# A two-block fp32 network on one Trainium2 core: transposes of normed tiles later in TensorE's order at two handoffs, and one modulation part moved to the second layer's mixer

## The chip, the cores and the metric

The kernel runs on one core of one Trainium2 chip. The metric is the device time of one execution in microseconds (us), as the median of several runs; lower is better. The program is one launch, with all weights in device memory (HBM) at its start.

## The reference, cut to what matters

A sequence of 256 rows of width 1024 goes through two hybrid layers (a mixer of pooling and sparse attention, then a feed-forward block with squared ReLU), and then through one block of a state-space branch, a dilated attention branch and another feed-forward block. All values are fp32. Two things of it bear on the change: each hybrid layer normalises its input and scales, shifts and gates it by six vectors that come from a matrix product with the conditioning vector `c`, and the last block ends its first half with a layer norm.

```python
def first_block(x, c, w_mod, b_mod, ...):
    c_act = jax.nn.silu(c)
    for l in range(DEPTH):                       # 2 layers
        mod = c_act @ w_mod[l] + b_mod[l]        # 1024 -> 6 * 1024
        x = hybrid_layer(x, mod, ...)

def hybrid_layer(x, mod, norm1, norm2, w_in, ..., w_out, w_ff1, w_ff2):
    shift1, scale1, gate1, shift2, scale2, gate2 = jnp.split(mod[:, None, :], 6, axis=-1)
    h = rms_norm(x, norm1) * (1.0 + scale1) + shift1
    proj = h @ w_in
    ...
    x = x + gate1 * mix
    h2 = rms_norm(x, norm2) * (1.0 + scale2) + shift2
    ff = jnp.square(jax.nn.relu(h2 @ w_ff1)) @ w_ff2
    return x + gate2 * ff

def second_block(x, ...):
    ...
    h = layer_norm(alpha * h + mix, ln1_g_2, ln1_b_2)
    f = jnp.square(jax.nn.relu(h @ w_up_2)) @ w_down_2
    return layer_norm(alpha * h + f, ln2_g_2, ln2_b_2)
```

## The kernel before

**Products.** The 256 rows are two tiles of 128 rows, called t=0 and t=1. To keep fp32 accuracy each operand is split into a high and a low part, and each product is three matmuls (`wh,hl`, `wl,hh`, `wh,hh`; the helper `mm` is L89). Weights are read once from HBM, 250 MB in all, in loads of 512 KB.

**Weights.** `Weights.load` (L130) takes a staging buffer `wst` (five of them, `nst=5`), issues the load on SyncE's DMA queue (SP, L136), lets ScalarE (ACT) copy it into a slot `wh` (L144) and VectorE (DVE) write the rest into a slot `wl` (L145). There are nine slots. A staging buffer is free again when its L145 is done, a slot when TensorE (PE) has used it.

**Modulation.** `mod_part` (L559) makes one of the six vectors of a layer. Its matrix is eight loads (L567) that go into the same five staging buffers. Each is multiplied by a column of `c` and added to `macc` by one DVE instruction (L569); in a part called with `modp1=99`, as those of the second layer's mixer are, the first of the eight goes over ACT (L571) and GpSimd (POOL, L572) instead. For a scale or a shift eight small matmuls then sum over the partitions (x16 in the profile, `tr<-cst,macc`) and DVE makes the columns `mcol` (L599, L601). For a gate, matmuls with `ones_r` spread the sum over all rows and ACT copies it to `mgate` (L589).

**Who does which part when.** The table `MODS` (L36) deals the parts to the stages: the first `mf0` of the list (0,5), (1,1), (1,0), (1,2), (1,3), (1,4) are made during layer 0's feed-forward, the rest during layer 1's mixer ((l,q): layer and vector). A part's steps are pulled by the weight loads: each load adds `W.rate` to a sum, and each whole unit takes one step (`Weights.load`, end).

**Handoffs.** Where a stage ends, its callback normalises tile t: `rms` (L609) squares on ACT (L613), makes the reciprocal root on POOL (L119) between two small DVE instructions, and scales on DVE (L617, `xn`). `to_fm` (L474) transposes `xn` on PE into the banks `tr` and `pv` (L479), applies scale and shift (DVE L488, ACT L486) and splits the result into `hh` and `hl` (L103, L106). `rms_fm` (L620) does not call `to_fm` at once: `later(n, fn)` (L184) puts it off by n ticks. In the last, wide pass of a stage one tick is two weight rows of one tile and one half, which is six matmuls. At the layer norm in the last block (`done_ln1`, L1646) `to_fm` is called at once.

**Order.** The program is written in this order, and a scheduler of the framework then fixes the order of each engine's instructions and of each queue's transfers. At run time every engine takes its instructions strictly in that order. The rope tables of layer 1 (L681 to L684, some 30 small POOL instructions), the pooling bands (L720, three loads) and the compression weights (L723, four loads) are also made at the handoff from layer 0 to layer 1.

Of the kernel before, what the change touches and what calls it, by code (L numbers as in the profile page):

```python
# [24 lines left out]
ALPHA = 2.0 ** 0.25  # L25

SZ = 1024
TU = dict(nst=5, tabc=2, nw=9, nt2=24, raw=1, krest=2, qrest=4, pool2=1, c2=3, c3=1, c4=1, ln=3, uv='uv', pre=[1], nv=5, nv1=0, nv0=0, u0=19.5, du=0.7, ub=2, uc=4, c0=32.5, dc=0.1, w0=36, dw=0.5, comp=22, pool=27, dpool=2, cmpa=32, cmpb=34, dcmp=2, e1=1, e0=1, pta=2, ahead=3, modp=3, rf=0.95, r0=0, r0b=2, r1=0.8, r1b=1.2, rs=14, raw_=4, qrest_=6, u0_=19.5, du_=1.0, comp_=22, pool_=26, cmpa_=31, cmpb_=35, nv_=0, nv0_=0, w0_=32, dw_=0.8, order2='v0 qk0 qk1 qk2 v1 B C x0 z0 x1 z1 x2 z2 x3 z3 g2 g3 pa g0 g1 ps', fm0=148, dfm=9, dts=8, dcd=30, par0=10, par1=40, d0=50, dd=2, db=3, dc2=5, ss0=70, ds=5.6, scb=5, sx=3, sr=6, sg=3.5, sy=3.5, sn=8, mf0=5, modp1=99, rf1=0.5, pool2_=3, c3_=2, c4_=3, nv1_=2, dpool_=2, dcmp_=1, dc_=0.4, cap=4, ub_=2.5, c0_=32.5, pta_=4)
NST, NW = TU['nst'], TU['nw']
NT2, NT4, NS5 = TU['nt2'], 5, 20  # L30

ORDER2 = TU["order2"].split()

MODS = {("mix", 0): ((0, 2), (0, 3), (0, 4)), ("ff", 0): [(0, 5), (1, 1), (1, 0), (1, 2), (1, 3), (1, 4)][:TU["mf0"]],  # L36
        ("mix", 1): [(0, 5), (1, 1), (1, 0), (1, 2), (1, 3), (1, 4)][TU["mf0"]:], ("ff", 1): ((1, 5),)}
CONV2 = {"x0": 0, "x1": 4, "x2": 8, "x3": 12, "B": 16, "C": 20}
# [23 lines left out]
def tile_two_blocks(ctx: ExitStack, tc: tile.TileContext, I, out, stop=None, dbg=None):  # L62
# [12 lines left out]
    def bank(tag):  # L75
        return pp.tile([128, 512], FT, name=tag, tag=tag, bufs={"acc": 4, "st": 2, "tr": 1, "pv": 1}[tag])

    def t2(shape, name, dt=FT):
        assert math.prod(shape[1:]) <= 512
        return bp.tile(shape, dt, name=name, tag="t2", bufs=NT2)  # L80
# [20 lines left out]
    def split(hi, lo, src, eng=None):  # L101
        if eng is A:
            A.activation(hi, src, AF.Copy)  # L103
        else:
            V.tensor_copy(hi, src)
        V.tensor_tensor(lo, src, hi, op=OP.subtract)  # L106
# [77 lines left out]
    def later(n, fn):  # L184

        waiting.append([n, fn])
# [284 lines left out]
    def new_h():  # L471
        return (xp.tile([128, 8, S], FR, name="hh", bufs=1), xp.tile([128, 8, S], FR, name="hl", bufs=1))

    def to_fm(t, xn, hi, lo, sc=None, sh=None, whole=None):  # L474

        for kb in range(2):
            b = bank(("tr", "pv")[kb])
            for k in range(4):
                T.transpose(b[:, k * 128:(k + 1) * 128], xn[kb][:, k * 128:(k + 1) * 128], ident)  # L479
            src = b.rearrange("p (a b) -> p a b", a=4)  # L480
            if sc is not None:
                hf = t2([128, 4, 128], "hf")
                for k in range(4):
                    kk = kb * 4 + k
                    if kb:
                        A.activation(hf[:, k], src[:, k], AF.Identity, bias=sh[:, kk:kk + 1], scale=sc[:, kk:kk + 1])  # L486
                    else:
                        V.tensor_scalar(hf[:, k], src[:, k], sc[:, kk:kk + 1], sh[:, kk:kk + 1], op0=OP.mult, op1=OP.add)  # L488
                src = hf
            ks, tsl = slice(kb * 4, kb * 4 + 4), slice(t * 128, t * 128 + 128)  # L490
            split(hi[:, ks, tsl], lo[:, ks, tsl], src, A)
            if whole:
                A.activation(whole[kb][:, :, tsl], src, AF.Copy)
# [3 lines left out]
    for l in range(DEPTH):  # L497
# [3 lines left out]
        if l == 0:  # L501
            for k in range(0, 8, 2):
                for n in "qk":
                    W.specs.append(([wi[:, k:k + 2, cols[n][0]:cols[n][1]]], 2, 512))
        for n in "qk" + TU["uv"]:
            if l or n in "uv":
# [6 lines left out]
    g2 = {}  # L513
# [43 lines left out]
    MC = {}  # L557
# [51 lines left out]
    def rms(t):  # L609
        ss = small.tile([128, 4], FT, name="ss", bufs=4)  # L610
        xn = [t2([128, 512], "xn") for _ in range(2)]
        for n in range(2):
            A.activation(xn[n], xs[t][:, n * 512:(n + 1) * 512], AF.Square, accum_out=ss[:, n:n + 1])  # L613
        V.tensor_scalar(ss[:, 2:3], ss[:, 0:1], D * EPS, ss[:, 1:2], op0=OP.add, op1=OP.add)
        rsqrt(ss[:, 3:4], ss[:, 2:3], 1)
        for n in range(2):
            V.tensor_scalar(xn[n], xs[t][:, n * 512:(n + 1) * 512], ss[:, 3:4], math.sqrt(D), op0=OP.mult, op1=OP.mult)  # L617
        return xn

    def rms_fm(l, q0, hi, lo, t):  # L620

        xn = rms(t)
        later(TU["ln"], lambda: to_fm(t, xn, hi, lo, MC[l, q0 + 1], MC[l, q0]))

    def first_mod(c):

# [36 lines left out]
    def hybrid_layer(l, hilo, between, done):  # L663
# [363 lines left out]
        def done1(t):  # L1027
            if not hi2lo2:
                W.until((l, 3), (l, 4))
                hi2lo2.extend(new_h())  # L1030
            rms_fm(l, 3, *hi2lo2, t)
# [111 lines left out]
    h1, h2_, hw = [], [], []  # L1143
# [5 lines left out]
    def done0(t):  # L1149
        if not h1:  # L1150
            W.until((1, 0), (1, 1))
            h1.extend(new_h())
        rms_fm(1, 0, *h1, t)

    hybrid_layer(0, h0, between0, done0)
    if stop == "l0":
        for t in range(2):
# [22 lines left out]
    def Q(n):  # L1180
        a, w = QC[n]
        return par2[:, a:a + w]

    hi, lo = h2_
# [413 lines left out]
    for i, it in enumerate(items):  # L1598
        g, t, sub = it
# [37 lines left out]
    def ln_stat(t):  # L1637
        mv = small.tile([128, 4], FT, name="bmv", bufs=2)
        V.bn_aggr(mv[:, 0:2], bst[t])
        V.tensor_scalar(mv[:, 2:3], mv[:, 1:2], NEPS / ALPHA ** 2, None, op0=OP.add)  # L1640
        rsqrt(mv[:, 3:4], mv[:, 2:3], 1)
        return mv

    hh = []

    def done_ln1(t):  # L1646
        if not hh:
            hh.extend(new_h())
        mv = ln_stat(t)
        xn = [t2([128, 512], "xn") for _ in range(2)]  # L1650
        for n in range(2):
            V.tensor_scalar(xn[n], xs[t][:, n * 512:(n + 1) * 512], mv[:, 0:1], mv[:, 3:4], op0=OP.subtract, op1=OP.mult)
        to_fm(t, xn, *hh, Q("ln1g"), Q("ln1b"))
        for n in range(2):
            ns = slice(n * 512, (n + 1) * 512)
            G.tensor_tensor(xs[t][:, ns], xn[n], rows["ln1_g_2"][:, n], op=OP.mult)
            G.tensor_tensor(xs[t][:, ns], xs[t][:, ns], rows["ln1_b_2"][:, n], op=OP.add)

    accs = {(t, n): bank("acc") for t in range(2) for n in range(2)}
    W.cap = NW  # L1660
    run(g2["o"].wide(act_o, accs, True, (ev_ln(0.5 / ALPHA), done_ln1)))

    def done_ln2(t):
# [122 lines left out]
```

## Time and profile before

| what | value |
|---|---|
| median of three runs | 1257.55 us (1257.31 to 1259.05) |
| the profiled execution | 1257.41 us |
| its span in the trace | 1255.6 us |
| PE busy | 1171.6 us, 93% of the span |
| DVE busy | 870.8 us, 69% |
| ACT busy | 646.3 us, 51% |
| POOL busy | 239.6 us, 19% |
| mean granted clock of PE | 0.981 |
| mean HBM rate | 197 GB/s |

The span runs from the first to the last instruction that the trace holds; the time of the execution has some 1.8 us around it. A time such as 387.76 is counted from the span's start. Busy shares are means over the program: the stages around the change are read from the timeline, in which each line is an instruction (or a merged run of equal ones) with its start, its duration, and in brackets the idle time of its engine ahead of it with what ended that. The granted clock is given as a share of full speed.

### The profile page before, as it was taken

The numbers are of one execution on the slowest core, as the hardware profiler recorded it, in microseconds if no ns is written. First come the engines' busy times: TensorE is split into PE (matmuls) and PEld (weight loads), VectorE is DVE, ScalarE is ACT, GpSimd is POOL, SyncE is SP. The second block draws the span as 40 slices with busy tenths as digits, with TensorE's granted clock in tenths as the row PEclk, the third lists the DMA queues.
The fourth block names the chain that finished last, engine by engine and source line by source line (L and its number), as shares of the span: only waits on it lengthen the run. The fifth ranks groups of instructions, "written<-read, shape, count | busy, mean of one in ns | idle before, by whom it ended". The sixth has DMA issues, their size and how long they took to land.

```text
span 1255.6 us, 18822 instructions
## 1 busy us (share of the span) xinstructions
PE 1171.6 (93%) x7060; PEld 1029.5 (82%) x7060; DVE 870.8 (69%) x1381; ACT 646.3 (51%) x1122; POOL 239.6 (19%) x233
## 2 busy tenths in 40 slices
PE   4778888999899999999999999999999999899997
PEld 3556776899787688788998999888888898799896
DVE  5777898888657857865444735688899767754544
ACT  4446355445454663655453443477689634645440
POOL 4553222212324101111010000001121102301101
PEclk9888999999999999999999999999999999999999
DMA  7855767889876633575655548465376753666640
GB/s 271 289 175 190 235 206 241 280 313 321 279 235 219 222 110 112 172 233 178 195 183 143 181 133 268 124 208 188 102 217 220 238 174 114 218 210 187 185 136 33
DMA packets 101778, 249.16 MB, mean 198 GB/s; under 512 B 9780, under 2 KB 15028, under 8 KB 101688
## 3 DMA queue, kind: packets, MB, share of 16 engines
q1 hardware_dynamic: 100904, 247.12, 61.3%
q8 instruction: 55, 0.90, 0.3%
q10 hardware_dynamic: 784, 0.85, 0.2%
q14 instruction: 35, 0.29, 0.1%
HBM read 246.03 MB, written 1.11 MB: 197 GB/s over the span
## 4 chain that ended last, share of the span: by engine, by line
PE 45%; issue 6%; DVE 3%; POOL 1%; ACT 1%; DMA 1%; SPq 0%; DVEq 0%; POOLq 0%; ACTq 0%
PE acc L89 30%; PE st L89 12%; PE pv L89 1%; DVE wl L145 1%; PE tr L89 1%; ACT wh L144 1%; DMA R<-rows 1%; POOL fr L399 1%; DMA wst<-in_w_up_dram 0%; PE st L1306 0%; DVE hl L106 0%; POOL yg L1492 0%; PE pv L479 0%; PE tr L479 0%; PE tr L1431 0%
## 5 line engine op out<-in xcount | busy, mean ns | idle before, releaser
L145 DVE TENSOR_TENSOR wl<-wst,wh 128x1024 fp32r<-128x1024 f32 (+3 forms) x324 | 403.5, 1257 | 152.6 <-ACT wh L144 150.9
L144 ACT ACTIVATE wh<-wst 128x1024 fp32r<-128x1024 f32 (+3 forms) x324 | 334.7, 1047 | 281.0 <-PE acc L89 94.0
L89 PE MATMUL st<-hh,wh 128*128 128x256 f32 x576 | 163.0, 283 | 0.0
L89 PE MATMUL st<-hl,wh 128*128 128x256 f32 x576 | 163.0, 283 | 0.0
L89 PE MATMUL st<-hh,wl 128*128 128x256 f32 x576 | 163.0, 283 | 0.0
L89 PE MATMUL acc<-wh,frl 128*128 128x512 f32 x384 | 152.3, 397 | 2.3 <-DVE frl L400 2.1
L89 PE MATMUL acc<-wl,frh 128*128 128x512 f32 x384 | 150.9, 393 | 0.0
L89 PE MATMUL acc<-wh,frh 128*128 128x512 f32 x384 | 150.6, 392 | 0.0
L399 POOL TENSOR_TENSOR fr<-fr 128x512 f32<-128x512 f32 x48 | 64.9, 1353 | 383.6 <-ACT frh L398 358.6
L89 PEld LDWEIGHTS st<-hl,wh 128*128 128x128 f32 x576 | 110.5, 192 | 0.7
L89 PEld LDWEIGHTS st<-hh,wl 128*128 128x128 f32 x576 | 110.5, 192 | 0.7
L89 PEld LDWEIGHTS st<-hh,wh 128*128 128x128 f32 x576 | 110.5, 192 | 0.0
L89 PE MATMUL acc<-wl,hh 128*128 128x512 f32 (+3 forms) x224 | 87.8, 392 | 11.0 <-DVE wl L145 11.0
L569 DVE SCALAR_TENSOR_TENSOR macc<-wst,cact,macc 128x1024 f32<-128x1024 f32 x70 | 92.7, 1325 | 5.7 <-DMA wst<-in_w_mod_dram 3.8
L89 PE MATMUL acc<-wh,hl 128*128 128x512 f32 (+3 forms) x224 | 88.8, 405 | 3.0 <-DVE hl L106 3.0
L89 PEld LDWEIGHTS acc<-wh,frl 128*128 128x128 f32 x384 | 73.0, 190 | 19.2 <-DVE frl L400 5.0
L89 PE MATMUL acc<-wh,hh 128*128 128x512 f32 (+3 forms) x224 | 87.2, 389 | 0.0
L89 PEld LDWEIGHTS acc<-wh,frh 128*128 128x128 f32 x384 | 72.7, 189 | 15.5
L89 PEld LDWEIGHTS acc<-wl,frh 128*128 128x128 f32 x384 | 73.1, 190 | 14.2
L89 PE MATMUL acc<-hh,wl 128*128 128x256 f32 x288 | 83.0, 288 | 0.4 <-DVE ym L1406 0.4
L89 PE MATMUL acc<-hl,wh 128*128 128x256 f32 x288 | 81.9, 284 | 0.0
L89 PE MATMUL acc<-hh,wh 128*128 128x256 f32 x288 | 81.4, 283 | 0.0
(332 smaller groups left out, 2327.0 us busy)
## 6 DMA issues: line engine op xcount, KB each, us to landing
wst<-in_w_ff_dram SPq DMA_DIRECT2D x128, 512.0 KB, 4.4
wst<-in_w_mod_dram SPq DMA_DIRECT2D x96, 512.0 KB, 4.7
wst<-in_w_in_dram SPq DMA_DIRECT2D x76, 512.0 KB, 4.7
wst<-in_w_up_dram SPq DMA_DIRECT2D x32, 512.0 KB, 4.0
wst<-in_w_down_dram SPq DMA_DIRECT2D x32, 512.0 KB, 3.8
wst<-in_w_out_dram SPq DMA_DIRECT2D x24, 512.0 KB, 4.5
ww<-in_w_in_dram SPq DMA_DIRECT2D x16, 512.0 KB, 5.3
R<-rows SPq DMA_DIRECT2D x32, 256.0 KB, 5.7
```

The costliest lines, as they stand in the source:

```text
L89: T.matmul(o, l, r, start=start, stop=stop, skip_group_check=True)
L144: A.activation(h[:, :kc * n], st[:, :kc * n], AF.Copy)
L145: V.tensor_tensor(l[:, :kc * n], st[:, :kc * n], h[:, :kc * n], op=OP.subtract)
L399: G.tensor_tensor(r, r, r, op=OP.mult)
L569: V.scalar_tensor_tensor(acc, st, cact[:, k:k + 1], acc, op0=OP.mult, op1=OP.add)
```

## The change

Three edits, of which the first changes where one of the parts is made:

1. `mf0` goes from 5 to 4. The part (1,3), with its eight loads, leaves layer 0's feed-forward and joins (1,4) in layer 1's mixer.
2. `rms_fm` takes the number of ticks as an argument; at the handoff from layer 0 to layer 1 tile t=0 waits 5 ticks in place of 3 (`ln0=5`).
3. In `done_ln1` the call of `to_fm` is put off by 3 ticks.

```diff
-TU = dict(..., ln=3, ..., mf0=5, ...)
+TU = dict(..., ln=3, ln0=5, ..., mf0=4, ...)
...
-    def rms_fm(l, q0, hi, lo, t):
+    def rms_fm(l, q0, hi, lo, t, wait=TU["ln"]):
         xn = rms(t)
-        later(TU["ln"], lambda: to_fm(t, xn, hi, lo, MC[l, q0 + 1], MC[l, q0]))
+        later(wait, lambda: to_fm(t, xn, hi, lo, MC[l, q0 + 1], MC[l, q0]))
...
-        rms_fm(1, 0, *h1, t)
+        rms_fm(1, 0, *h1, t, TU["ln0"] if t == 0 else TU["ln"])
...
-        to_fm(t, xn, *hh, Q("ln1g"), Q("ln1b"))
+        later(TU["ln"], lambda: to_fm(t, xn, *hh, Q("ln1g"), Q("ln1b")))
```

**The order at the handoff.** On SP's queue, from the last feed-forward loads of layer 0 to layer 1's input weights (`in_w_in`), before the change:

```order
L136 DMA wst<-in_w_ff_dram 128x1024 x8
L136 DMA wst<-in_w_in_dram 128x2x512 x3
L564 DMA macc<-in_b_mod_dram 1x1024
L136 DMA wst<-in_w_in_dram 128x2x512
L567 DMA wst<-in_w_mod_dram 128x1024 x8
L136 DMA wst<-in_w_in_dram 128x2x512 x5
L720 DMA band<-in_bands_dram 128x512 x3
```

and after it:

```order
L136 DMA wst<-in_w_ff_dram 128x1024 x8
L136 DMA wst<-in_w_in_dram 128x2x512 x4
L567 DMA wst<-in_w_mod_dram 128x1024 x12
L720 DMA band<-in_bands_dram 128x512 x3
L723 DMA w_3479<-in_w_dram 128x512
L723 DMA w_3481<-in_w_dram 128x512
L723 DMA w_3483<-in_w_dram 128x512
L723 DMA w_3485<-in_w_dram 128x512
L567 DMA wst<-in_w_mod_dram 128x1024 x4
L136 DMA wst<-in_w_in_dram 128x2x512 x8
```

Sixteen modulation loads, twelve in a row and four after the bands and the compression weights, stand ahead of the fifth load of `in_w_in`, where eight stood; no modulation load stands among the last feed-forward loads any more.

On PE, after the first 24 matmuls of layer 1 (its first four weight loads with tile t=0), before:

```order
L89 MATMUL acc<-wh,hh 128x512
L89 MATMUL tr<-cst,macc 128x64 x8
L89 MATMUL acc<-wh,hl 128x512
L89 MATMUL acc<-wl,hh 128x512
L89 MATMUL acc<-wh,hh 128x512
```

and after, with the part (1,3) as the first `tr<-cst,macc`, (1,4) as the second, and `xn` that of tile t=1:

```order
L89 MATMUL acc<-wh,hh 128x512
L89 MATMUL tr<-cst,macc 128x64 x8
L479 MATMUL pv<-cst,xn 128x128 x4
L89 MATMUL tr<-cst,macc 128x64 x8
L89 MATMUL acc<-wh,hl 128x512
L89 MATMUL acc<-wl,hh 128x512
L479 MATMUL tr<-cst,xn 128x128 x4
```

Both parts and one transpose of tile t=1 now stand ahead of the products with the fifth load of `in_w_in`; before, one part stood there and the transposes came nine matmuls later.

On DVE, from the norm of tile t=1 (`xn`, L617) to the first `wl` of the fifth `in_w_in` load, after the change:

```order
L617 TENSOR_SCALAR xn<-x_89,ss 128x512 x2
L569 SCALAR_TENSOR_TENSOR macc<-wst,cact,macc 128x1024
L599 TENSOR_TENSOR mcol<-tr,parc_86 128x8
L569 SCALAR_TENSOR_TENSOR macc<-wst,cact,macc 128x1024 x6
L145 TENSOR_TENSOR wl<-wst,wh 128x1024
```

Before, all eight L569 of the one part stood ahead of that L617, among the last feed-forward work; now seven of the sixteen stand behind it. On POOL the change puts the L572 of the second part, which stood nowhere, between the L119 of tile t=0 and the rope tables, and the L119 of tile t=1, on which this L617 waits, stays behind the tables.

## Rows read from the trace of the kernel before

**Rows 1.** The page, part 1: busy time of each engine.

```profile
PE 1171.6 (93%) x7060; PEld 1029.5 (82%) x7060; DVE 870.8 (69%) x1381; ACT 646.3 (51%) x1122; POOL 239.6 (19%) x233
```

**Rows 2.** Windows: busy time by engine, PE's granted clock, DMA share, GB/s.

```profile
372.00:400.00 28.00, 24.27 (x103) 19.74 (x103) 20.40 (x27) 9.78 (x17) 16.37 (x32) 0.94 0.55 173
...
430.00:480.00 50.00, 48.68 (x314) 41.41 (x315) 34.18 (x111) 26.60 (x75) 2.93 (x5) 1.00 0.41 127
```

**Rows 3.** Timeline of PE, layer 0's feed-forward, around its longest wait.

```profile
318.47 0.39 PE L89 MATMUL acc<-wl,frh 128*128 128x512 f32 x1
318.70 0.40 PE L89 MATMUL acc<-wh,frh 128*128 128x512 f32 x1
323.15 0.47 PE L89 MATMUL tr<-mal,ones_r 128*128 128x512 f32 x1 [4.05 <-ACT mgate L589]
323.82 0.63 PE L89 MATMUL acc<-wh,frl 128*128 128x512 f32 x1
...
326.81 0.45 PE L89 MATMUL acc<-wl,frh 128*128 128x512 f32 x1
```

**Rows 4.** Timeline of ACT in the same place.

```profile
318.36 1.06 ACT L144 ACTIVATE wh<-wst 128x1024 fp32r<-128x1024 f32 x1 [4.59 <-DMA wst<-in_w_ff_dram]
```

**Rows 5.** Timeline of SP's queue, layer 0's feed-forward to the handoff.

```profile
312.48 0.33 SPq L567 DMA_DIRECT2D wst<-in_w_mod_dram  x1
...
335.83 19.59 SPq L136 DMA_DIRECT2D wst<-in_w_ff_dram  x12
...
367.55 22.01 SPq L567 DMA_DIRECT2D wst<-in_w_mod_dram  x8
392.38 9.33 SPq L136 DMA_DIRECT2D wst<-in_w_in_dram  x5
```

**Rows 6.** Timeline of PE, the matmuls of the part (1,3).

```profile
351.83 1.89 PE L89 MATMUL tr<-cst,macc 128*128 128x64 f32 x16
353.53 0.48 PE L89 MATMUL acc<-wh,frl 128*128 128x512 f32 x1
```

**Rows 7.** Timeline of PE at the handoff from layer 0 to layer 1.

```profile
387.76 0.63 PE L479 MATMUL tr<-cst,xn 128*128 128x128 f32 x4 [2.60 <-DVE xn L617]
...
396.44 0.39 PE L89 MATMUL acc<-wh,hl 128*128 128x512 f32 x1
...
412.11 0.69 PE L89 MATMUL acc<-wh,hl 128*128 128x512 f32 x1 [1.89 <-DVE hl L106]
```

**Rows 8.** Timeline of DVE at the same handoff.

```profile
389.12 1.36 DVE L488 TENSOR_SCALAR hf<-tr,mcol 128x128 f32<-128x128 f32 x4
...
391.07 1.28 DVE L569 SCALAR_TENSOR_TENSOR macc<-wst,cact,macc 128x1024 f32<-128x1024 f32 x1
...
401.24 1.23 DVE L145 TENSOR_TENSOR wl<-wst,wh 128x1024 fp32r<-128x1024 f32 x1
...
405.02 0.88 DVE L617 TENSOR_SCALAR xn<-x,ss 128x512 f32<-128x512 f32 x2
```

**Rows 9.** Timeline of ACT at the same handoff.

```profile
396.08 1.06 ACT L144 ACTIVATE wh<-wst 128x1024 fp32r<-128x1024 f32 x1 [0.34 <-DMA wst<-in_w_in_dram]
```

**Rows 10.** Timeline of POOL at the same handoff.

```profile
373.32 2.40 POOL L572 TENSOR_TENSOR macc<-macc,wst 128x1024 f32<-128x1024 f32 x1 [0.81 <-ACT wst L571]
...
387.07 0.64 POOL L681 TENSOR_TENSOR tab<-par,cst 128x32 f32<-128x32 f32 x2
...
389.27 0.45 POOL L681 TENSOR_TENSOR tab<-par,cst 128x32 f32<-128x32 f32 x2
...
391.19 1.25 POOL L683 TENSOR_TENSOR tab<-par,cst 128x32 f32<-128x32 f32 x1
...
398.35 1.22 POOL L683 TENSOR_TENSOR tab<-par,cst 128x32 f32<-128x32 f32 x1
...
402.67 0.57 POOL L119 TENSOR_TENSOR ss<-ss,half 128x1 f32<-128x1 f32 x1 [1.21 <-DVE ss L614]
```

**Rows 11.** Timeline of PE at the layer norm of the last block.

```profile
1072.63 0.66 PE L479 MATMUL tr<-cst,xn 128*128 128x128 f32 x4 [2.51 <-DVE xn L1652]
```

More of the change, by code (lines that the diff above doesn't have):

```diff
@@ L27 @@
 SZ = 1024
-TU = dict(nst=5, tabc=2, nw=9, nt2=24, raw=1, krest=2, qrest=4, pool2=1, c2=3, c3=1, c4=1, ln=3, uv='uv', pre=[1], nv=5, nv1=0, nv0=0, u0=19.5, du=0.7, ub=2, uc=4, c0=32.5, dc=0.1, w0=36, dw=0.5, comp=22, pool=27, dpool=2, cmpa=32, cmpb=34, dcmp=2, e1=1, e0=1, pta=2, ahead=3, modp=3, rf=0.95, r0=0, r0b=2, r1=0.8, r1b=1.2, rs=14, raw_=4, qrest_=6, u0_=19.5, du_=1.0, comp_=22, pool_=26, cmpa_=31, cmpb_=35, nv_=0, nv0_=0, w0_=32, dw_=0.8, order2='v0 qk0 qk1 qk2 v1 B C x0 z0 x1 z1 x2 z2 x3 z3 g2 g3 pa g0 g1 ps', fm0=148, dfm=9, dts=8, dcd=30, par0=10, par1=40, d0=50, dd=2, db=3, dc2=5, ss0=70, ds=5.6, scb=5, sx=3, sr=6, sg=3.5, sy=3.5, sn=8, mf0=5, modp1=99, rf1=0.5, pool2_=3, c3_=2, c4_=3, nv1_=2, dpool_=2, dcmp_=1, dc_=0.4, cap=4, ub_=2.5, c0_=32.5, pta_=4)
+TU = dict(nst=5, tabc=2, nw=9, nt2=24, raw=1, krest=2, qrest=4, pool2=1, c2=3, c3=1, c4=1, ln=3, ln0=5, uv='uv', pre=[1], nv=5, nv1=0, nv0=0, u0=19.5, du=0.7, ub=2, uc=4, c0=32.5, dc=0.1, w0=36, dw=0.5, comp=22, pool=27, dpool=2, cmpa=32, cmpb=34, dcmp=2, e1=1, e0=1, pta=2, ahead=3, modp=3, rf=0.95, r0=0, r0b=2, r1=0.8, r1b=1.2, rs=14, raw_=4, qrest_=6, u0_=19.5, du_=1.0, comp_=22, pool_=26, cmpa_=31, cmpb_=35, nv_=0, nv0_=0, w0_=32, dw_=0.8, order2='v0 qk0 qk1 qk2 v1 B C x0 z0 x1 z1 x2 z2 x3 z3 g2 g3 pa g0 g1 ps', fm0=148, dfm=9, dts=8, dcd=30, par0=10, par1=40, d0=50, dd=2, db=3, dc2=5, ss0=70, ds=5.6, scb=5, sx=3, sr=6, sg=3.5, sy=3.5, sn=8, mf0=4, modp1=99, rf1=0.5, pool2_=3, c3_=2, c4_=3, nv1_=2, dpool_=2, dcmp_=1, dc_=0.4, cap=4, ub_=2.5, c0_=32.5, pta_=4)
 NST, NW = TU['nst'], TU['nw']
```

## The prediction

> **What bounds the kernel now.** The busy times on the profile's page come first: PE has 1171.6 us, 93% of the span, and no other engine comes near [rows 1]. So time can be won or lost where PE stands idle or runs at its lower clock. The list of waits gives the places, and the timeline shows each in turn; the reader should look there for the bracket ahead of a PE instruction, and for what its releaser had itself been waiting for. Three places are touched.
>
> First, layer 0's feed-forward. PE stops after 318.70 and goes on at 323.15, 4.05 us idle, for the copy of a gate (`mgate`) by ACT [rows 3]. ACT was late because it stood 4.59 us at a weight copy whose load had not landed [rows 4]. That load was late because modulation loads of the part (1,3), the one at 312.48 the latest, had taken staging buffers [rows 5]: such a buffer is given back by DVE's L569, and those stood behind other work. After the wait the matmuls come 0.43 us apart (323.82 to 326.81, seven steps) where 318.47 to 318.70 are 0.23: half clock [rows 3].
>
> Second, the handoff to layer 1. PE is idle 2.60 us for `xn` of tile t=0 and 1.89 us for `hl` of tile t=1 [rows 7], and the window around the first has a granted clock of 0.94 [rows 2], full speed (2.4 GHz) with some microseconds at the half level (1.2 GHz).
>
> Third, the layer norm of the last block, with 2.51 us for `xn` of the second tile [rows 11].
>
> **The change part by part.**
>
> *Out of layer 0's feed-forward.* With no loads of (1,3) among them, the feed-forward loads get all five buffers, and the copy on which ACT stood is not late. The gate's copy still stands behind a weight copy whose slot PE frees shortly before, so I leave about 0.2 us of the 4.05: -3.85. Seven steps 0.2 us too long, and the one before them, go too: -1.6. The part's own matmuls hold PE from 351.83 to 353.53 [rows 6]: -1.7, since at their new place PE is waiting anyway. Together -7.15 us. All times that follow are on the clock of the trace before, that is, without this shift.
>
> *Tile t=0 later at the handoff.* Nine matmuls more stand ahead of the transposes, 9 x 0.23 = 2.1 us [rows 3], so PE idles about 0.6 us in place of 2.60, and the low clock (28 us at 0.94, a loss of 1.7 [rows 2]) stays away. The first products of layer 1, which began at 396.44 [rows 7], begin at about 393. It is worth 3.5 us there, but what follows swallows it.
>
> *Into the handoff.* The order puts both parts, (1,3) and (1,4), on PE ahead of the products with the fifth `in_w_in` load. PE's first 24 matmuls take 24 x 0.23 = 5.5 us and end near 398.5. From then it waits for the last of 16 modulation loads, where before it waited for 8. The chain to that:
> - The first eight go, as the eight before, through two buffers: 22.0 us from 367.55 [rows 5], 2.75 us each. The other three hold `in_w_in` loads.
> - The ninth takes the buffer of the second `in_w_in` load, which DVE gives back after L488 (to 390.5 [rows 8]) and the L145 behind it, 1.23 each [rows 8]: between 391.7 and 392.9; I take the latter.
> - A lone load took 3.7 us (392.38 issued, its copy at 396.08 [rows 5, 9]): landed 396.6. Being the first of its part it goes over ACT, about as long as the 1.06 us of a copy [rows 9], and POOL, 2.40 us [rows 10]: 400.2.
> - On POOL this stands *ahead* of the rope tables, and the root for tile t=1 behind them. The price of the tables in this place is not shown. Before, the same instructions took from 387.07 to the L683 at 398.35, 11.3 us, of which nine took only 1.92 (389.27 to 391.19) [rows 10]. The slow L683 at 391.19 takes 1.25 us exactly beside an L569 of DVE [rows 8, 10]. Some 27 at the quick price are 5.8 us. In this place DVE soon has nothing to do but wait for this root, so I take 6: 406.2. Upper end 11.3.
> - Root 0.57 [rows 10] and `xn` 0.88 [rows 8]: about 408, with semaphores. Only behind it stand the L569 of the remaining seven loads: 7 x 1.28 [rows 8] = 9. The last two loads go into buffers that the first of these free, and land in step. So 417; PE's matmuls of the second part, partly at the low clock, to 419.5.
> - The four `in_w_in` loads behind them come in buffers freed by those L569, and their L145 stand behind tile t=1's L488 and L106. The last is through at about 427.3, and PE's last six matmuls of this tile near 428.7.
>
> Tile t=1 began its own products at 412.11 [rows 7]. Now it can at 428.7: +16.6, a little less for clock: **+16.5**. The 1.89 us for `hl` is in that difference, since the transposes are long done by then.
>
> Nothing gives it back. From 430 to 480 PE is busy 48.68 of 50 us at full clock [rows 2]; a later start simply shifts this.
>
> The lower end of this term is the transfers alone: ninth load at 392.9, eight at 19.59/12 = 1.63 us each [rows 5], 13.0 us, then bands and compression weights (1.75 MB, 3.5 loads, 5.7 us), 2.1 us to land and one L569 give 415; then four loads, 6.5 us, a copy, an L145 and six matmuls, 3.7: 424, +12. With the ninth load at 391.7, +10.5. The upper end has the slow tables: +21.5. I take the middle value, because on its path POOL and DVE follow one another and each price has a row.
>
> *What the Trainium skill says to the tables.* The page "SBUF — State Buffer", section "SBUF: two separate sides", has VectorE and GpSimd share a port pair under an exclusive lock, which a VectorE instruction with two operands in SBUF holds against a GpSimd one that reads SBUF. By that the tables run at the quick price wherever VectorE stands idle, and the sum is the one taken; if the pieces were slow of themselves, it would be 5 us more. The coincidence at 391 us agrees.
>
> *Layer norm.* The first tile's transposes come six matmuls later, its small wait goes. The second tile's come two matmuls earlier on PE, but DVE reaches its statistics one L145 (1.23 us [rows 8]) sooner, so its 2.51 shrinks by under a microsecond; a later transpose gives back some 0.4. Bounds 0 and -1.5; I take -0.7.
>
> **The sum.** -7.15 + 16.5 - 0.7 = +8.65 us. The profiled execution took 1257.41, which is 0.14 under the median of the runs shown, so 1257.55 + 8.65 = **1266.2 us**.
>
> **The rivals.**
>
> *Everything lands in time (faster).* If the loads ran at the pace of the feed-forward's twelve, 16 x 1.63 = 26 us from 367.55 [rows 5], they would be there at about 396, before PE comes to the parts near 398.5. That is the point from which it decides: the last L569 done by then. Then only gains are left: 7.15, 3.5 for tile t=0, 1.89 for tile t=1 with as much lost clock as at the first, 1.7, and 0.7: 1242.5 us. For it speaks that the transfers have room (DMA share 0.55 [rows 2]). Against it, that eight loads took 22 us, being tied to two buffers and to DVE, and that seven L569 stand in DVE's order behind a norm whose root came at 402.67 [rows 10]. Chance 0.11.
>
> *The transfers' end alone.* The tables are done early or the ninth load comes sooner, and the handoff costs +10.5 to +12: 1260.2 to 1261.7 us. For it speaks that POOL's spans are rough; against it that the L119 stands behind two long pieces of POOL. Chance 0.14.
>
> *The first wait does not go.* The change would then not do what it can at layer 0's feed-forward: the gate's copy on ACT still stands behind weight copies, and if one of those waits for a load or a slot as before, 5.45 us of gain fall away: 1271.7 us. For it: ACT's order there has one more weight copy ahead of the gate's. Against it: the load waited for was late only by the buffers [rows 4, 5]. Chance 0.12.
>
> **How the numbers follow.** The forecast, with tables between 5 and 9 us, has 0.58: 1262 to 1271. Some 0.05 is left for mixtures between the first rival and no change. A measurement of this kernel tells about 0.2%, 2.5 us, from no change. Faster by more: the first rival and a part of the mixtures, 0.13. Within it: the rest of these and the cheapest end of the second rival, 0.08. Slower: 0.79. The range leaves out the first rival and the mixtures, some 0.17, and little above: 1259 to 1273.
>
> **What would show it.** In the new profile: no wait of PE on `mgate` beyond half a microsecond near 311 to 316, and no half clock behind it; at the handoff two long waits of PE in the list of waits, on `xn` of tile t=1 (about 9 us) and on `macc` from L569 (about 8), in place of 1.89 on `hl`; on POOL a second L572 ahead of the tables and the tables quick after it; tile t=1's products beginning about 9 us later than before; equal distances from there to the last block. Wrong would be a wait on `macc` that is short or missing (first rival), or the handoff long because the loads themselves land late, with the tables done early (second).

## The result, and the profile after

The changed kernel took 1271.14 us in the median of four runs (1267.71 to 1276.08), the kernel before 1257.43 beside it (1255.04 to 1259.05). The ratio is 1.0108, 95% interval [1.0078, 1.0138]: by that, slower by some 13.6 us. A second measurement, told below as the last experiment, gave 1267.5 and 1.0083 [1.0057, 1.0109]. The forecast was 1266.2, +8.65.

The page of the changed kernel, part 1, answers to [rows 1]. PE has 3 us more to do than before, in a span 10 us longer. The execution in this trace took 1267.71 us, the shortest of the four, so of the 13.6 us it can show 10:

```profile
PE 1174.6 (93%) x7060; PEld 1032.2 (82%) x7060; DVE 867.2 (69%) x1380; ACT 647.6 (51%) x1123; POOL 236.9 (19%) x234
```

Where the time came and went is read by lining up the same instructions in both traces. These are four of ACT's in the timeline of the kernel before: one early in layer 0's feed-forward, the first square of the norm that ends it, the first square behind layer 1's mixer, and one in the last feed-forward:

```profile
298.36 0.63 ACT L398 ACTIVATE frh<-fr 128x512 fp32r<-128x512 f32 x1
...
377.67 0.63 ACT L613 ACTIVATE xn<-x 128x512 f32<-128x512 f32 x1 [4.43 <-DVE x L1020]
...
502.98 0.63 ACT L613 ACTIVATE xn<-x 128x512 f32<-128x512 f32 x1 [6.55 <-DVE x L1020]
...
1088.24 0.63 ACT L398 ACTIVATE frh<-fr 128x512 fp32r<-128x512 f32 x1
```

and the same four in the changed kernel's:

```profile
298.26 0.63 ACT L398 ACTIVATE frh<-fr 128x512 fp32r<-128x512 f32 x1
...
372.88 0.63 ACT L613 ACTIVATE xn<-x 128x512 f32<-128x512 f32 x1 [4.76 <-DVE x L1020]
...
515.32 0.63 ACT L613 ACTIVATE xn<-x 128x512 f32<-128x512 f32 x1 [6.69 <-DVE x L1020]
...
1097.90 0.63 ACT L398 ACTIVATE frh<-fr 128x512 fp32r<-128x512 f32 x1
```

The differences are -0.1, -4.8, +12.3 and +9.7 us. So the feed-forward gave 4.7, the stretch of handoff and mixer took 17.1, and the long stretch from 503 to 1088, with the layer norm near its end, gave 2.7.

In the timeline of PE at the handoff, the two waits of [rows 7] are gone, and three longer ones stand in their place:

```profile
382.62 0.66 PE L479 MATMUL tr<-cst,xn 128*128 128x128 f32 x4
...
388.55 0.50 PE L89 MATMUL acc<-wh,hl 128*128 128x512 f32 x1 [0.72 <-DVE hl L106]
...
397.11 3.54 PE L89 MATMUL tr<-cst,macc 128*128 128x64 f32 x16 [2.82 <-DVE macc L569]
404.15 1.11 PE L479 MATMUL pv<-cst,xn 128*128 128x128 f32 x4 [3.50 <-DVE xn L617]
413.35 3.65 PE L89 MATMUL tr<-cst,macc 128*128 128x64 f32 x16 [8.09 <-DVE macc L569]
```

PE waits for the first part, for the norm of tile t=1, and for the second part. The sixteen small matmuls of a part take 3.5 us where they took 1.89 [rows 6]: the granted clock fell. The windows that answer to [rows 2]:

```profile
372.00:400.00 28.00, 24.42 (x111) 19.90 (x110) 21.06 (x27) 9.32 (x18) 7.44 (x17) 0.95 0.66 196
400.00:430.00 30.00, 18.41 (x77) 15.47 (x77) 22.15 (x32) 12.30 (x20) 6.81 (x18) 0.65 0.83 277
430.00:480.00 50.00, 47.29 (x280) 38.86 (x280) 34.82 (x107) 30.82 (x68) 5.71 (x7) 1.00 0.46 144
```

From 400 to 430 PE had 18 of 30 us to do and a mean clock of 0.65. From 430 on it is full, so nothing is given back.

The chain behind these waits, engine by engine. ACT's L571 of the ninth modulation load, which it had to wait for:

```profile
391.88 1.15 ACT L571 ACTIVATE wst<-wst,cact 128x1024 f32<-128x1024 f32 x1 [2.03 <-DMA wst<-in_w_mod_dram]
```

POOL's L572, the first rope table, the last but a few, and the root of tile t=1, in answer to [rows 10]:

```profile
393.11 2.86 POOL L572 TENSOR_TENSOR macc<-macc,wst 128x1024 f32<-128x1024 f32 x1 [11.07 <-ACT wst L571]
395.93 1.42 POOL L681 TENSOR_TENSOR tab<-par,cst 128x32 f32<-128x32 f32 x2
...
402.33 0.26 POOL L682 TENSOR_TENSOR tab<-par,cst 128x32 f32<-128x32 f32 x1
402.53 0.59 POOL L119 TENSOR_TENSOR ss<-ss,half 128x1 f32<-128x1 f32 x1
```

and DVE, which stood 6.10 us for that root and then had seven L569 to do, in answer to [rows 8]:

```profile
403.16 0.94 DVE L617 TENSOR_SCALAR xn<-x,ss 128x512 f32<-128x512 f32 x2 [6.10 <-POOL ss L119]
404.01 1.27 DVE L569 SCALAR_TENSOR_TENSOR macc<-wst,cact,macc 128x1024 f32<-128x1024 f32 x1
405.20 0.15 DVE L599 TENSOR_TENSOR mcol<-tr,parc 128x8 f32<-128x8 f32 x1
405.31 7.89 DVE L569 SCALAR_TENSOR_TENSOR macc<-wst,cact,macc 128x1024 f32<-128x1024 f32 x6
```

405.31 + 7.89 is 413.2, and PE goes on at 413.35.

The first of the three waits, 2.82 us for the first part, has a cause of its own. The last L569 of that part took 3.24 us where the one before it took 1.28, beside POOL's L572, which ended at 395.97:

```profile
392.48 1.28 DVE L569 SCALAR_TENSOR_TENSOR macc<-wst,cact,macc 128x1024 f32<-128x1024 f32 x1
...
393.81 3.24 DVE L569 SCALAR_TENSOR_TENSOR macc<-wst,cact,macc 128x1024 f32<-128x1024 f32 x1
```

It does not move the end, since tile t=1's `xn` comes later still.

### The profile page after: what moved, and what is told of

The parts are those of the page before. It is cut to its first block, busy times and chain, and to the rows that moved or that the text cites. A ratio compares the mean times of both kernels' runs of the same rounds, so it can differ in the third digit from the quotient of the medians.

```text
span 1265.6 us, 18824 instructions
## 1 busy us (share of the span) xinstructions
PE 1174.6 (93%) x7060; PEld 1032.2 (82%) x7060; DVE 867.2 (69%) x1380; ACT 647.6 (51%) x1123; POOL 236.9 (19%) x234
## 4 chain that ended last, share of the span: by engine, by line
PE 46%; DVE 4%; issue 3%; DMA 2%; ACT 2%; POOL 1%; SPq 0%; DVEq 0%; POOLq 0%; ACTq 0%
PE acc L89 32%; PE st L89 12%; DVE wl L145 1%; DMA R<-rows 1%; PE pv L89 1%; PE tr L89 1%; DMA dil<-in_dbias_dram 1%; POOL fr L399 1%; DMA wst<-in_w_up_dram 0%; ACT wh L144 0%; DVE hl L106 0%; ACT R L1468 0%; DVE G L1457 0%; POOL yg L1492 0%; PE pv L479 0%
## 5 line engine op out<-in xcount | busy, mean ns | idle before, releaser
L399 POOL TENSOR_TENSOR fr<-fr 128x512 f32<-128x512 f32 x48 | 64.6, 1347 | 380.2 <-ACT frh L398 353.4
L89 PE MATMUL acc<-wl,hh 128*128 128x512 f32 (+3 forms) x224 | 88.8, 397 | 11.3 <-DVE wl L145 11.3
L569 DVE SCALAR_TENSOR_TENSOR macc<-wst,cact,macc 128x1024 f32<-128x1024 f32 x69 | 90.8, 1316 | 6.6 <-DMA wst<-in_w_mod_dram 3.9
```

Source lines behind the costliest of these rows:

```text
L89: T.matmul(o, l, r, start=start, stop=stop, skip_group_check=True)
L399: G.tensor_tensor(r, r, r, op=OP.mult)
L569: V.scalar_tensor_tensor(acc, st, cact[:, k:k + 1], acc, op0=OP.mult, op1=OP.add)
```

## The experiments

The theory at this point: sixteen modulation loads that come in one burst at the handoff make the loss; the later transposes are a gain or nothing. The rival: the moved transposes make it. Of the long line `TU` the diffs show the changed entries alone.

**e1: the change without its first edit.**

```diff
-mf0=4
+mf0=5
```

> The change without its first edit: the part (1,3) stays in layer 0's feed-forward, the transposes of tile t=0 and those of the layer norm are later. My theory is that the modulation loads at the handoff are what made the change slower, and that later transposes gain: about 2.5 us at the layer norm, as the changed kernel's trace shows there, and about 1 us at the handoff (the 2.60 us wait and its low clock go, but tile t=1's norm still stands behind the rope tables). So 3.5 us faster than the kernel before, 1254 us against 1257.4, and 13 to 17 us faster than the change. A rival: the later transposes themselves cost at the handoff; then this stays at or above 1260.

Measured: 1256.75 us, before 1255.44, ratio 1.0005 [0.9987, 1.0022]: no difference, 2.7 us above my number. The two edits on transposes cost nothing, so the rival falls, but they gain nothing that the runs can tell either: at the handoff the waits that go come back for `macc` and for tile t=1's `xn` (0.80 and 1.31 us in its trace). Between the second and the third mark of ACT this trace took 125.5 us, the kernel before 125.3.

**e2: the first edit alone.**

```diff
-ln0=5
+ln0=3
-        later(TU["ln"], lambda: to_fm(t, xn, *hh, Q("ln1g"), Q("ln1b")))
+        to_fm(t, xn, *hh, Q("ln1g"), Q("ln1b"))
```

> The first edit alone: the part (1,3) moves to layer 1's mixer, all transposes stay where they were before the change. My theory: this alone carries the loss. Layer 0's feed-forward gains 5.6 us, the handoff loses 17 beyond what PE had gained by then, so +12.5 us against the kernel before if the profiled pair is taken, up to +16 by the medians: 1270 to 1274 us, that is 2 to 3 us slower than the whole change, the part that the layer norm gives. The wait of PE on macc of L569 stands in its profile as in the change's, some 8 us. A rival: the loss comes from moving the transposes of tile t=0; then this is faster than before by some 5 us, about 1252.

Measured: 1269.74 us, ratio 1.0122 [1.0089, 1.0155]: the loss as expected, 0.3 us under the range. That this kernel would be 2 to 3 us slower than the whole change is not shown (1271.14 and 1267.5 us). Its list of waits of PE at the handoff has `macc` and `xn` again:

```profile
PE tr L89 <- DVE macc L569: 8.6, 2, 6.8
PE pv L479 <- DVE xn L617: 6.0, 1, 6.0
PE tr L479 <- DVE xn L617: 2.2, 1, 2.2
```

The move alone carries the loss.

**e4: no POOL in the chain.**

```diff
-    W.extra.extend(mod_part(*m, TU["modp1"]) for m in MODS["mix", 1])
+    W.extra.extend(mod_part(*m, V) for m in MODS["mix", 1])
```

> All three edits, and the first load of each part in layer 1's mixer is taken by DVE's L569 like the others, so ACT's L571 and POOL's L572 go from the handoff. My theory is that the chain ran over POOL: ninth load, L571, L572, rope tables, root of tile t=1, xn, and only then the seven L569. Without L572 the tables start at once after the root of tile t=0 (near 382 in the changed kernel's trace) and are done before tile t=1 is ready, so xn comes near 395 in place of 404 and the last L569 some 6 us sooner, bounded by the loads: 5 to 7 us faster than the change, about 1262 to 1265. A rival: the transfers alone set the end; then less than 2 us is won.

Measured: 1265.03 us, ratio 1.0077 [1.0047, 1.0106], against 1.0108 and 1.0083 of the whole change: in the place forecast, but the intervals overlap, and what POOL costs is not settled by time. The trace says more. Tile t=1's norm comes 4.4 us sooner, though this execution was 1.2 us later up to the handoff. It is not the 9 us expected: the tables, which now run beside a busy DVE, took longer, as POOL's timeline shows (the first two and, after 27 in all, the next):

```profile
382.71 0.64 POOL L681 TENSOR_TENSOR tab<-par,cst 128x32 f32<-128x32 f32 x2
...
395.40 1.23 POOL L683 TENSOR_TENSOR tab<-par,cst 128x32 f32<-128x32 f32 x1
```

The next limit is the transfers, as DVE's timeline shows:

```profile
398.81 0.88 DVE L617 TENSOR_SCALAR xn<-x,ss 128x512 f32<-128x512 f32 x2 [0.96 <-POOL ss L119]
...
407.16 5.24 DVE L569 SCALAR_TENSOR_TENSOR macc<-wst,cact,macc 128x1024 f32<-128x1024 f32 x4 [3.56 <-DMA wst<-in_w_mod_dram]
```

The last four loads stand behind the bands and compression weights. The chain over POOL and the transfers end close together: the stretch of handoff and mixer is still 14.2 us longer than in the kernel before, where the whole change has 17.1.

**e3: the loads spread over the mixer.** The code shows why sixteen loads come at once: the sum `due` keeps growing while no part is left, and pays out everything at the next load. With it set to zero the order has ten `in_w_in` loads in a row.

```diff
-    W.rate = TU["r1"]
+    W.rate, W.due = TU["r1"], 0.0
-r1=0.8, r1b=1.2
+r1=0, r1b=2
```

> All three edits, but the modulation loads of layer 1's mixer do not come in one burst. In Weights.load the sum 'due' keeps growing while no part is left, so that at the start of layer 1 it pays out all steps of both parts at the first weight load. Here due is set to zero at that point, the rate to 0 until step 14 of the mixer (r1=0) and to 2 from there (r1b=2). The order then has ten in_w_in loads in a row and the sixteen modulation loads among the later ones. My theory (place, not number, of these loads is the cost): PE's three waits at the handoff go, the gains of feed-forward (5.6), of tile t=0 (3.5), of tile t=1 (up to 3.5) and of the layer norm (2.5) remain: 1242 to 1246 us, some 13 us under the kernel before. A rival (the mixer has no room for sixteen loads; they delay the attention instead): 1255 us or more, with new waits of PE between 430 and 500.

Measured: 1258.95 us, ratio 1.0042 [1.0022, 1.0062]. My theory that place alone is the cost falls; the rival holds. The burst was the cost *at the handoff*: by DVE's L793, which ended its first head, this kernel led the one before by 11.9 us (417.42 before). But by the first square after the mixer (501.27 against 502.98) 1.7 us were left. Its window over the mixer, and under it that of the kernel before over about the same work:

```profile
418.00:520.00 102.00, 96.76 (x576) 80.90 (x575) 85.11 (x203) 52.56 (x129) 13.91 (x10) 0.97 0.57 185
```

```profile
430.00:532.00 102.00, 98.09 (x588) 81.96 (x589) 76.48 (x196) 53.30 (x134) 11.32 (x11) 1.00 0.43 135
```

DVE is busy 85 of 102 us in place of 76, PE waits more, and the clock is 0.97. So the loads cost time in the mixer too; which engine sets it, this run does not show.

**e5: half of the spread loads over ACT and POOL.**

```diff
 (e3, and)
-modp1=99
+modp1=2
```

> The spread version of before (e3) with every second modulation load of layer 1's mixer taken by ACT (L571) and POOL (L572) in place of DVE's L569 (modp1=2). In e3 the lead of 12 us over the kernel before that stood at 418 us in the trace was lost until 546, in a stretch where DVE was busy 18 to 19 of 20 us. My theory: DVE is what gives out there. Eight L569 fewer are 10 us of DVE time, of which I expect 5 to 8 back on the path: 1251 to 1254 us where e3 had 1259 and the kernel before 1255.4. A rival: the loss comes from the transfers or from PE's own matmuls for the parts; then the time stays within 2 us of e3's. Another: POOL and DVE hinder one another at the two-operand adds, then it is slower than e3.

Measured: 1265.33 us, ratio 1.0081 [1.0056, 1.0106], slower than e3. Fewer L569 did not help (six fewer, 8 in place of 14, where I had counted eight); the trace speaks for the third possibility. That DVE's busy time counts for nothing does not follow, since the six instructions more on POOL may have cost more than was saved, and six L571 more on ACT came with them, which no run separates. POOL's timeline has

```profile
408.56 3.06 POOL L572 TENSOR_TENSOR macc<-macc,wst 128x1024 f32<-128x1024 f32 x1 [0.78 <-ACT wst L571]
...
425.30 2.35 POOL L572 TENSOR_TENSOR macc<-macc,wst 128x1024 f32<-128x1024 f32 x1
```

and DVE's, in the same places,

```profile
409.29 2.48 DVE L700 TENSOR_TENSOR sq<-sq,krt 128x128 f32<-128x128 f32 x1
...
425.36 2.44 DVE L703 TENSOR_TENSOR sq<-sq,hr 128x128 f32<-128x128 f32 x1 [0.36 <-POOL hr L119]
```

Both DVE instructions take about 0.28 us elsewhere. Each ends with the L572 beside it (408.56 + 3.06 = 11.62 and 409.29 + 2.48 = 11.77; 427.65 and 427.80). PE waits behind them, 2.29 us at 413.16 and 1.95 at 427.94. The first of these two pairs is in e3 as well (2.47 us in L700). The Trainium skill, page "SBUF — State Buffer", section "SBUF: two separate sides", says that the two engines share a port pair under an exclusive lock for the whole instruction. The trace agrees, and here in the direction that the prediction had not looked at: POOL stops DVE.

**e8: one part spread, half of it over POOL.**

```diff
 (e5, and)
-mf0=4
+mf0=5
```

> The part (1,3) stays in layer 0's feed-forward, as in e1, and the one part (1,4) of layer 1's mixer is spread over later loads (due to zero, r1=0, r1b=2) with every second load on ACT and POOL. My theory: without any modulation load at the handoff PE's waits there go (some 6 us), four L569 and four L572 in the mixer cost some 2 to 3, the layer norm gives 2.5: 1249 to 1252 us. A rival: the mixer loses per part what e3 showed for two (14 us), that is 7 for one; then 1255 or more.

Measured: 1263.89 us, ratio 1.0072 [1.005, 1.0094]. The rival holds, and more than it said: even one part in the mixer, with four L572, loses more than had been won up to there: a lead of 8.8 us at the key copy L742 (416.41 before) is a lag of 6.8 at the copies of the next handoff (L486, the first at 510.63 before); 4 us of it come only there, where PE waits 4.12 us for `xn`.

**e9: the spread loads all on DVE.**

```diff
 (e3, and)
-    W.extra.extend(mod_part(*m, TU["modp1"]) for m in MODS["mix", 1])
+    W.extra.extend(mod_part(*m, V) for m in MODS["mix", 1])
```

> The spread version (e3) with all sixteen loads of layer 1's mixer on DVE's L569, none on ACT and POOL; e5, the same with eight on POOL, was 6 us slower than e3. In the trace of e8 three of DVE's small two-operand instructions took 2.3 to 2.5 us in place of 0.3 to 0.7, each beside a L572 of POOL. My theory: a two-operand instruction of DVE stands still while a L572 runs. Taking out the last two L572 then wins 1 to 4 us on e3, 1255 to 1258 us, though DVE has two more L569 (2.6 us). A rival: DVE's busy time is what counts; then it is slower than e3 by 1 to 3 us, 1260 to 1262.

Measured: 1262.26 us (1252.71 to 1271.5), ratio 1.0049 [1.0017, 1.0081]. Inconclusive: the interval, 1257.6 to 1265.7 us, holds e3's ratio, all of the rival's numbers and the upper edge of my theory's. The execution in its trace was the longest of the twelve, so the trace is not read for what the mixer costs.

**e6: the opposite of the change.**

```diff
-mf0=4
+mf0=6
```

> The opposite of the change: mf0=6, both (1,3) and (1,4) are made in layer 0's feed-forward, and no modulation load stands at the handoff; transposes later as in the change. My theory: at the handoff the waits for xn and hl go with their low clock, some 7 us; the layer norm gives 2.5; the feed-forward has DVE and transfer room for eight more loads in its second half and loses at most 3. So 1246 to 1250 us, some 5 to 9 under the kernel before. A rival: the eight loads take staging buffers among the feed-forward's and stop PE there as the part (1,3) did before; then 1253 or more.

Measured: 1248.41 us, before 1255.3, ratio 0.9949 [0.9932, 0.9966]: faster. Where the kernel before waited for `xn` and `hl`, PE's list of waits from 372 to 430 has only

```profile
PE tr L798 <- DVE qr L793: 2.0, 2, 1.0
PE acc L89 <- DVE frl L400: 0.8, 1, 0.8
```

and the window of the second half of the feed-forward shows where the loads went, with PE full at full clock, and the transfers at a share of 0.93:

```profile
340.00:372.00 32.00, 31.92 (x209) 28.74 (x207) 25.67 (x25) 16.23 (x20) 5.42 (x4) 1.00 0.93 329
```

**e10: all parts in the feed-forward, nothing else.**

```diff
 (the kernel before, and)
-mf0=5
+mf0=6
```

> All six parts in layer 0's feed-forward (mf0=6) and nothing else: the transposes stand where they were before the change. It divides the 7 us that e6 won. My theory: e6's trace has neither the wait for xn of tile t=0 (2.60 us before, with its low clock) nor that for hl of tile t=1; the first is due to the later transposes, the second to the missing modulation loads, whose DVE work stood ahead of tile t=1's norm. So about half is left: 1251 to 1253 us where the kernel before has 1255.4. A rival: the modulation loads alone made both waits; then 1248 to 1250 as e6.

Measured: 1251.29 us, ratio 0.9961 [0.9938, 0.9983]. The time is where my theory had it, but its interval takes in e6's ratio, and the trace, though of the shortest of the twelve runs, speaks for the rival: without any later transpose the wait for `xn` of tile t=0 is 0.4 us in place of 2.60.

```profile
PE tr L798 <- DVE qr L793: 1.4, 2, 1.1
PE tr L479 <- DVE xn L617: 0.4, 1, 0.4
```

In the kernel before, DVE's steps of that norm had stood behind an L569 that waited for its load:

```profile
385.05 1.29 DVE L569 SCALAR_TENSOR_TENSOR macc<-wst,cact,macc 128x1024 f32<-128x1024 f32 x1 [1.24 <-DMA wst<-in_w_mod_dram]
...
387.13 0.88 DVE L617 TENSOR_SCALAR xn<-x,ss 128x512 f32<-128x512 f32 x2 [0.67 <-POOL ss L119]
```

Taking the loads away removes it. The stretch of handoff and mixer settles it: it is 8.5 us shorter than in the kernel before here, and 8.4 in e6.

**e11: a gate's sum in two banks.**

```diff
 (e6, and)
-                b = bank("tr")
+                b = bank(("tr", "pv")[n])
                 mm(b, ones_r, al, True)
```

> e6 with the second half of a gate's sum in the bank pv in place of tr, so that PE need not wait until ACT has copied the first half. In the traces so far PE waited for that copy in layer 0's feed-forward, with the part (1,3) there 4.05, 1.19, 2.33, 4.27 and 2.48 us and without it 1.64, 0.15, 1.40, 2.45 and 1.47. My theory: the wait belongs to the one bank, not to the loads of (1,3); it goes altogether here, with its low clock, and the time falls by 2 to 4 us from e6's 1248.4: 1244.5 to 1246.5. A rival: the copy is late for another reason that stops the next user of the bank instead; then no change.

Measured: 1245.74 us, ratio 0.9922 [0.9896, 0.9948], the fastest kernel of all, 9.8 us under the one before. But it does not show my theory: the wait for the gate's copy is gone, and another has come 50 us later, which ACT's casts, waiting for feed-forward loads, make:

```profile
370.07 0.80 PE L89 MATMUL acc<-wh,frl 128*128 128x512 f32 x1 [4.61 <-DVE frl L400]
```

Its lead over e6 lies within the intervals, and its cause is open.

**e7: the layer norm's edit alone.**

```diff
 (the kernel before, and)
-        to_fm(t, xn, *hh, Q("ln1g"), Q("ln1b"))
+        later(TU["ln"], lambda: to_fm(t, xn, *hh, Q("ln1g"), Q("ln1b")))
```

> The third edit alone: the layer norm's transposes three ticks later, everything else as before the change. My theory, from the changed kernel's trace: 2.5 us faster than the kernel before, 1253 us against 1255.4. What I had put down for it in the prediction was 0.7. A rival: what the later transposes win at the layer norm comes back as a later wait in the feed-forward behind it; then no difference.

Measured: 1256.28 us, ratio 0.9997 [0.9978, 1.0015]: no difference, the rival's side. In the trace 1.1 us are won from the first tile's norm (DVE's first L1652) to the mark of ACT at 1088: the second wait for `xn` is 1.58 us in place of 2.51 [rows 11], and a transpose behind it waits a little longer. That wait is 1.27 to 1.72 us in the eleven traces with this edit and 2.18 to 2.64 in the three without. A gain of this size lies inside the interval of the runs.

**e12: the change once more.**

> The changed kernel once more, unchanged, to see which of its terms repeat. From the profiled pair: layer 0's feed-forward 4.5 us won, the handoff 17.0 lost, the layer norm 2.5 won. The handoff's loss rests on a fixed order and should come out within 1.5 us of 17 again, with the three waits of PE there 13 to 16 us in all; the feed-forward's share hangs on a wait that was anything from 0.15 to 2.45 us in the traces of e2 to e5, so it should lie between 3 and 6; the layer norm between 1 and 2.5. The time: 1267 to 1271 us, 12 to 15 above the kernel before. If the handoff's loss is far smaller this time, the chain that I put down for it is not what sets it.

Measured: 1267.5 us, before 1256.46, ratio 1.0083 [1.0057, 1.0109]. The marks of ACT as above:

```profile
298.09 0.63 ACT L398 ACTIVATE frh<-fr 128x512 fp32r<-128x512 f32 x1
...
371.73 0.63 ACT L613 ACTIVATE xn<-x 128x512 f32<-128x512 f32 x1 [4.77 <-DVE x L1020]
...
514.16 0.63 ACT L613 ACTIVATE xn<-x 128x512 f32<-128x512 f32 x1 [6.61 <-DVE x L1020]
...
1097.31 0.63 ACT L398 ACTIVATE frh<-fr 128x512 fp32r<-128x512 f32 x1
```

Against the kernel before: -0.3, -5.9, +11.2 and +9.1. The feed-forward gave 5.7, the handoff took 17.1 again, the rest gave 2.1. PE's waits at the handoff repeat to 0.2 us:

```profile
PE tr L89 <- DVE macc L569: 10.9, 2, 8.1
PE pv L479 <- DVE xn L617: 3.3, 1, 3.3
```

## Why the prediction was right

**The handoff** (+16.5 forecast, 17.1 and 17.1 in two traces). The measured stretch takes in the mixer as well. Each link was there in the forecast order: ninth load, L571, L572, tables, root, `xn`, seven L569, the part's matmuls. The two waits of PE that were to show it, about 9 us for `xn` and 8 for `macc`, came as 3.50 and 8.09: the wait of 2.82 us for the first part, which the forecast did not have, and that part's matmuls at the lower clock (3.54 us) filled the rest, without moving the end. The tables took 395.93 to 402.53, 6.6 us where I had taken 6: quick, apart from the first piece, as DVE stood idle. The upper end of 11.3 us, of tables as slow as before, did not occur; in e4, with DVE at work beside them, the same 27 pieces took 12.7 us. e4 adds that the two candidates for the limit, POOL's chain and the transfers, lie close: without POOL the transfers stop DVE for 3.56 us, and the stretch costs 14.2 us where the rival of the transfers' end alone had 10.5 to 12.

This term repeats in every trace. From ACT's second mark to its third it took 125.3, 125.5 and 125.3 us with eight loads in a burst (before, e1, e7), 142.4, 142.4 and 142.7 with sixteen (the change, e12, e2), and 116.9, 116.8 and 117.0 with none (e6, e10, e11). Later transposes are in some of each group and make no difference of more than 0.3 us.

**The feed-forward** (-7.15 forecast, -4.7 and -5.7 in two traces). This term was mis-sized. I let the wait of 4.05 us [rows 3] shrink to 0.2; PE's timeline in the changed kernel still has

```profile
322.01 0.47 PE L89 MATMUL tr<-mal,ones_r 128*128 128x512 f32 x1 [1.64 <-POOL fr L399]
```

though at full clock; the copy of the gate on ACT ended at 321.86, beside the L399 that is named there, after a weight copy that began at 320.32. The deeper fault is that the 4.05 was one execution's. In the trace of e1, with the loads of (1,3) in their old place, the same wait was

```profile
318.86 0.47 PE L89 MATMUL tr<-mal,ones_r 128*128 128x512 f32 x1 [1.19 <-ACT mgate L589]
```

and in e7, also with them there, it was 4.27. The six traces with (1,3) in the feed-forward and one bank have 4.05, 1.19, 4.27, 2.33, 2.48 and 1.87, the seven without 1.64, 0.15, 1.40, 2.45, 1.47, 1.38 and 3.47: means of 2.70 and 1.71. So the loads made it longer by some 1.0 us in the mean, not by 3.85, and with such a scatter even that is not clear of nothing. The cause I gave, buffers held by the loads of (1,3), is at most the smaller part; the rest was not settled. The whole stretch, from ACT's first mark to its second, says the same: 79.3 us in the kernel before, 76.3, 78.5 and 75.1 in e1, e7 and e8 with the same loads in it, and 72.0 to 74.6 in the seven traces without those of (1,3). That is 3.7 us less in the mean, half of the forecast.

**Tile t=0.** Forecast 3.5 us won at the handoff and swallowed behind it. In the trace the wait for `xn` was zero, layer 1's first products began at 388.55, which is 393.3 when the 4.8 us gained ahead are added (forecast about 393), and it was swallowed. e1 shows it from the other side: kept without the move, it brings no measurable time.

**The layer norm** (-0.7, bounds 0 and -1.5). e7 has -1.1 in the trace and none in the runs. From the first tile's norm to the mark at 1088 the eleven traces with this edit took 33.2 to 34.7 us, the three without (before, e2, e10) 35.4 to 35.9: 1.7 less in the mean, so this term was put too small. The 2.7 and 2.1 of the change over the longer stretch from 503 to 1088 are not the edit's alone: e10, without it, has 1.1 there, and e1, with it, lost 1.1.

**The sum.** +8.65 stood against +13.6 and +10.4 by the ratios of the runs; the second interval takes the forecast in, the first lies above it. In the trace of the result the three stretches and the start add up to +9.7: the feed-forward gave 2.5 us less than forecast, the layer norm's stretch 2.0 more, and the handoff cost 0.6 more. That the first two nearly cancel was luck. The 3.4 us by which the median of those four runs lies above the traced one are in no trace. The rival "everything lands in time" did not occur: PE's last wait ended at 413 in this trace, 418 on the clock of the forecast, and not before 398.5. Of the forecast's sentence on the mixer, "nothing gives it back" held. "The first wait does not go" came in part: 1.64 of 4.05 us stayed, without the low clock.

## What to carry to other kernels

Work that is off the critical path has to go where its engine, its buffers and its queue all have slack at once: here a second eight loads cost 17 us at a handoff and the first eight 8.4, while a feed-forward stretch became 3.7 us shorter in the mean without eight of them and 1.9 longer with eight more (two traces). Spread over an attention stretch, sixteen took back 10 of the 12 us by which e3 led ahead of it. Before moving work towards its consumer, read which in-order engine stands between, and what is queued there behind a wait. And a wait of one profiled execution is a sample: before building a term on it, see it in a second trace.

## What the runs showed of the hardware that I had not expected

An elementwise add of POOL over 128x1024 with both operands in SBUF holds up a two-operand instruction of DVE until it ends: 2.48 and 2.44 us in place of 0.28 (e5), and an L569 of 3.24 us in place of 1.28 at the handoff of the changed kernel. Work given to a nearly idle POOL was dearer here than the same work on a busy DVE: e5 with eight such adds took 1265.33 us, e3 with two 1258.95. That this hold-up alone makes the difference is not shown: e9, with none, took 1262.26 us in runs that scatter by 19.

Over three waits of PE of 2.8 to 8.1 us in a row, with little between them, the granted clock was at its half level, 1.2 GHz, for longer than around one wait: the mean of 400 to 430 was 0.65, where the kernel before, with a wait of 1.89 us there, has 0.94:

```profile
400.00:430.00 30.00, 27.30 (x127) 21.51 (x126) 24.60 (x55) 20.66 (x35) 6.66 (x6) 0.94 0.79 271
```
